# The modulation's products side by side in four column groups of TensorE, in float32

## The chip, the cores and the metric

The kernel runs on one core of one Trainium2 chip. The metric is the device time of one execution in microseconds (us), from the first to the last instruction and what lies around it. Engines are named as the profile names them: PE is TensorE's matmul, PEld its weight load, DVE is VectorE, ACT ScalarE, POOL GpSimd, SP the engine that issues the DMAs.

## The reference, cut to what matters

A network of two blocks runs over 256 rows of 1024 channels. The first block has two layers, a Hyena layer (gated long convolution by a Fourier transform) and an attention layer. Each layer is modulated by two conditioning vectors, one for the latent rows and one for the context rows:

```
sc_lat, sc_ctx = silu(c), silu(c_ctx)                     # 1024 numbers each
for i in range(2):
    sh, sc, gt       = split(sc_lat @ ada_w[i] + ada_b[i], 3)
    sh_c, sc_c, gt_c = split(sc_ctx @ ada_w[i] + ada_b[i], 3)
    h_lat = rms_norm(x_lat, g[i]) * (1 + sc) + sh         # the same for h_ctx with the _c parts
    x_lat = x_lat + gt * mixer(h_lat, ...)
```

`ada_w` is 2 x 1024 x 3072 in float32, 25 MB in all, so the modulation multiplies two rows by a large matrix. The second block (recurrences, window attention and a mixture of experts whose rows are gathered by index) takes the larger part of the time and isn't touched by the change.

## The kernel before, in words

The activations of the first block lie transposed in `hT`, eight chunks of 128 channels by 512 rows. Large products are made by three matmuls (`mm3`, lines 115 to 117) on operands that are split into a rounded part (`hi`, by ACT, line 77) and the rest (`lo`, by DVE or POOL, line 78), both read by TensorE in the type float32r. Each weight tile of 128 x 1024 (512 KB) comes by one DMA into a ring of four raw tiles `w` (`load`, line 93), and is split into a ring of three split tiles (`weights`).

The function `ada` makes the modulation of one layer in six column blocks `nb` of 512. A block takes four tiles of `ada_w` (`h` = 0 to 3), and each tile holds two chunks `c` of the 1024 input channels, so a block sums eight products in one PSUM bank. The stationary operand is the conditioning vectors' chunk, 128 x 2; the moving operand is the weight, 128 x 512. ACT copies the sum to `row`, TensorE turns it by four transposes, and DVE adds the bias into `mod0` (layer 0) or `mod1` (layer 1). `ada` gives control back after each tile, so that a caller can place one step of it between other work.

There are two ways through it:
- with `raws`: float32 matmuls straight from the raw tile, two columns (`cr`). Blocks 0 to 3 of layer 0 go this way ahead of the Hyena layer (raw tiles of their own, `aw`, 16 of them); so do blocks 3 to 5 of layer 1, at the end of the Hyena layer and behind it, out of the ring `w`.
- without: the weight is split as all others are, and the stationary operand `cs` has four columns (the two vectors' `hi` and `lo`). So a tile takes four float32r matmuls. Blocks 4 and 5 of layer 0 and blocks 0 to 2 of layer 1 go this way, one step (one tile) at a time between the products of the Hyena layer: the generator `aside`, 20 steps, called from `project(g + 1, (1,), ...)`.

Ahead of the Hyena layer `modulated` makes `hT` from `x`, `mod0` and the row norms, first for chunks 0 to 3 (it needs blocks 0 and 2), then for chunks 4 to 7 (blocks 1 and 3). Behind the Hyena layer the row norms of `x` are summed (`RmsRows.rows`), blocks 4 and 5 of layer 1 are finished, `modulated` makes `hT` for the attention layer, and its first products (keys and values, `at_kv`) follow.

The program isn't issued in the order in which it is written: the framework places instructions on each engine's queue by the order of the program as a priority and by a simulation of when each is ready. On the chip each queue then runs in that fixed order. All DMAs of weights are issued by SP, in order; one that has to wait for a free tile of a ring holds up those behind it.

Of the kernel before, what the change touches and what calls it, by code (L numbers as in the profile page):

```python
# [10 lines left out]
F32 = mybir.dt.float32  # L11
F32R = mybir.dt.float32r
# [3 lines left out]
AF = mybir.ActivationFunctionType  # L16
ALU = mybir.AluOpType
# [3 lines left out]
P = 128  # L21
D = 1024
NKD = D // P
# [125 lines left out]
def bc(ap, dim, n):  # L149

    v = ap.unsqueeze(dim)
    shape = list(v.shape)
    shape[dim] = n
    return v.broadcast_to(shape)
# [67 lines left out]
    nc.scalar.activation(out, x, AF.Sin)  # L222


def ada(k, io, l, cv, mod, nbs, rows, raws=None):

    nc = k.nc
    m = 2 if raws else 4
    for nb in nbs:
        ps = k.bank("A")
        for h in range(4):
            src = io["ada_w"][l, nb, h]
            w = (raws(src) if raws else k.weights(src, [2, 512]))
            for j in range(2):
                c = 2 * h + j
                if raws:  # L240
                    k.mm(ps[:2, :], cv[0][:, c, :], w[:, j * 512:(j + 1) * 512], c == 0, c == NKD - 1)
                else:
                    k.mm(ps[:4, :], cv[1][:, c, :], w.hi[:, j, :], c == 0, False)
                    k.mm(ps[:4, :], cv[1][:, c, :], w.lo[:, j, :], False, c == NKD - 1)
            if h < 3:
                yield
        row = rows([P, 512])[:m]
        nc.scalar.copy(row, ps[:m, :])
        pm = k.bank("B")
        for j in range(4):  # L250
            nc.tensor.transpose(pm[:, m * j:m * j + m], row[:, j * P:(j + 1) * P], k.ident[:m, :m])
        o = mod[:, 4 * nb:4 * nb + 4, :]
        pm = pm[:, :4 * m].rearrange("p (a b) -> p a b", b=m)
        nc.vector.tensor_tensor(o, pm[:, :, 0:2], bc(k.adab[:, l, 4 * nb:4 * nb + 4], 2, 2), ALU.add)
        if not raws:
            nc.vector.tensor_tensor(o, pm[:, :, 2:4], o, ALU.add)
        yield


# [1087 lines left out]
@with_exitstack  # L1347
def tile_model(ctx: ExitStack, tc: tile.TileContext, io, out):
    nc = tc.nc
    k = Kit(ctx, tc)  # L1350
    k.out = out
    k.ident = k.con.tile([P, P], F32, tag="ident", name="ident")
    make_identity(nc, k.ident)
    k.ones = k.con.tile([P, P], F32, tag="ones", name="ones")
    nc.vector.memset(k.ones, 1.0)
    k.half = k.con.tile([P, 1], F32, tag="half", name="half")
    nc.vector.memset(k.half, -0.5)
    banks = ExitStack()
    k.psum(banks, "1", {"A": 4, "B": 2, "C": 2})
    with ExitStack() as blk:  # L1360
        k.stage(blk, "1", 1024, 4, 3)
        b1 = blk.enter_context(tc.tile_pool(name="b1", bufs=1))
        x = b1.tile([P, NKD, 512], F32, tag="x", name="x")
        hT = k.new_split(b1, [P, NKD, 512], "hT1")
        cr = b1.tile([P, NKD, 2], F32, tag="cr", name="cr")
        nc.sync.dma_start(cr, io["cT"])
        cs = b1.tile([P, NKD, 4], F32R, tag="cs", name="cs")
        nc.scalar.activation(cr, cr, AF.Silu)
        nc.scalar.activation(cs[:, :, 0:2], cr, AF.Copy)
        nc.vector.tensor_tensor(cs[:, :, 2:4], cr, cs[:, :, 0:2].bitcast(F32), ALU.subtract)  # L1370
        mod0 = k.con.tile([P, 24, 2], F32, tag="mod0", name="mod0")
        mod1 = k.con.tile([P, 24, 2], F32, tag="mod1", name="mod1")
        ada_steps = lambda *a: ada(k, io, a[0], (cr, cs), *a[1:])

        def adas(*a):
            for _ in ada_steps(*a):
                pass

        with ExitStack() as c1:
            p1 = c1.enter_context(tc.tile_pool(name="hy", bufs=1))  # L1380
            hs = k.new_split(p1, [64, SEQ], "fhs")
            dft_f = k.new_split(p1, [P, 2, 2, 128], "dff")
            dft_i = k.new_split(p1, [P, 2, 2, P], "dfi")
            with ExitStack() as c2:
                fp = c2.enter_context(tc.tile_pool(name="filt", bufs=1))
                mlp = filter_mlp(k, fp, io, hs)
                rms = RmsRows(k, fp, 512)
                frow = lambda s: fp.tile(s, F32, tag="ada_row", name=k.uid("ada_row"))
                raws = lambda src: k.load(src, 1024, pool=fp)
                for i, _ in enumerate(ada_steps(0, mod0, (0, 2), frow, raws)):  # L1390
                    nc.sync.dma_start(x[:, i, :], io["xT"][:, i, :])
                    if i == 0:
                        k.adab = k.const(io["ada_b"], [P, 2, 24], "adab")
                        ng = k.const(io["norm_g"], [P, 2, NKD], "ng")
                    if i in (1, 3, 5):
                        next(mlp)
                    rms.add(x[:, i, :], fp.tile([P, 512], F32, tag="rms_q", name=k.uid("rms_q"), bufs=2))
                next(mlp, None)
                rb = rms.rows()
                adas(0, mod0, (1, 3), frow, raws)  # L1400
                modulated(k, fp, hT, x, mod0, ng[:, 0, :], rb, range(4))
                modulated(k, fp, hT, x, mod0, ng[:, 0, :], rb, range(4, 8))

            def load_dft():
                for d, n, w in ((dft_f, "dft_f", 512), (dft_i, "dft_i", 512)):
                    raw = k.raw.tile([P, 1024], F32, tag="w", name=k.uid("w"))[:, :w]
                    nc.sync.dma_start(raw, io[n])
                    k.split_into(d.view(lambda a: a.rearrange("p a b c -> p (a b c)")), raw)

            with ExitStack() as c2:  # L1410
                rms = RmsRows(k, p1, 512)

                hp = c2.enter_context(tc.tile_pool(name="hyg", bufs=1))
                hrow = lambda s: hp.tile(s, F32, tag="hcv", name=k.uid("ada_row"))

                def aside():
                    yield from ada_steps(0, mod0, range(4, 6), hrow)
                    yield from ada_steps(1, mod1, range(3), hrow)

                hyena(k, io, x, hT, hs, {}, dft_f, dft_i, mod0, hp, aside(), ada_steps(1, mod1, (3,), hrow, lambda src: k.load(src, 1024)), rms, load_dft)  # L1420
            with ExitStack() as c2:
                rp = c2.enter_context(tc.tile_pool(name="rm1", bufs=1))
                more = ada_steps(1, mod1, range(4, 6), lambda s: rp.tile(s, F32, tag="ada_row", name=k.uid("ada_row")), lambda src: k.load(src, 1024))
                for _ in range(3):
                    next(more)
                rb = rms.rows()
                for _ in more:
                    pass
                modulated(k, rp, hT, x, mod1, ng[:, 1, :], rb, range(NKD))
        with ExitStack() as c2:  # L1430
            at = c2.enter_context(tc.tile_pool(name="at", bufs=1))
            gqa(k, io, x, hT, mod1, at)
        k.iota = k.const(io["iota"], [P, P], "iota")
        k.tri = k.const(io["tri"], [P, P], "tri")
        k.msk = k.const(io["mask"], [P, 3, P], "msk")
        po = [k.bank("A") for _ in range(4)]
        for t in range(2):
            for dh in range(2):
                for j in range(4):
                    nc.tensor.transpose(po[2 * t + dh][:, j * P:(j + 1) * P], x[:, 4 * dh + j, t * P:(t + 1) * P], k.ident)  # L1440
    k.stage(ctx, "2", 1024, RAWS, 3)
    b2 = ctx.enter_context(tc.tile_pool(name="b2", bufs=1))
    h = [b2.tile([P, D], F32, tag=f"h{t}", name=f"h{t}") for t in range(2)]
    for t in range(2):
        for dh in range(2):
            nc.scalar.copy(h[t][:, dh * 512:(dh + 1) * 512], po[2 * t + dh])
    banks.close()
    k.psum(ctx, "2", {"G": 2, "M": 2, "C": 2, "D": 2})
    second = Second(k, io, b2, h)
    for t in range(2):  # L1450
        second.stats(t, 0, None)
        second.scaled(t)
    second.experts()
# [136 lines left out]
```

## Time and profile before

| what | value |
|---|---|
| runs before, median of 3 (lowest to highest) | 2750.16 us (2749.62 to 2754.34) |
| the profiled execution, its own time | 2752.02 us |
| its span, first to last instruction | 2750.3 us |
| PE busy over the span | 2364.6 us (86%) |
| DVE, ACT, POOL busy | 2075.2 (75%), 1294.2 (47%), 1055.5 us (38%) |
| mean granted TensorE clock | 0.958 |

The trace covers the whole span, 0 us being the first instruction. The stages that matter here: the prologue from 0 to about 44 us, the Hyena layer from there to about 610 us, the passage to the attention layer from 580 to 640 us. A busy share is a mean over a stage. The ends of matmuls are modelled, so that neighbours overlap in the records; the distance from start to start is what a matmul takes from TensorE.

### The profile page before, as it was taken

How to read it: one execution, taken by the hardware profiler on the slowest of the kernel's cores; microseconds unless marked ns; L12 is line 12 of the kernel's file. 1: busy time of each engine (PE TensorE's matmuls, PEld its weight loads, DVE VectorE, ACT ScalarE, POOL GpSimd, SP SyncE). 2: the span in 40 equal slices, each digit the busy share in tenths (PEclk: the TensorE clock that was granted, in tenths of full speed). 3: DMA queues.
4: the chain of work that ended last, by engine and by line, in shares of the span. 5: the costliest groups of instructions: out<-in, count | busy, mean ns of one | idle time of the engine just before them, and what ended most of it. 6: DMA issues, size and time to landing. Idle time of an engine off the chain costs nothing. (4 is left out here: it accounts for less than half of the span.)

```text
span 2750.3 us, 30013 instructions
## 1 busy us (share of the span) xinstructions
PE 2364.6 (86%) x8930; PEld 1463.6 (53%) x8930; DVE 2075.2 (75%) x4579; ACT 1294.2 (47%) x2960; POOL 1055.5 (38%) x844
## 2 busy tenths in 40 slices
PE   8999999999998786788978888987788998777776
PEld 4788888857888454445533344544344544322222
DVE  6788887766887876799758589867689966964444
ACT  4444444434554664467534366734366753322222
POOL 0322223221210443544445455544444454343332
PEclk9999999999999797899999999999999999899999
DMA  6333332224333554999899999999999999899997
GB/s 245 123 106 112 111 108 90 79 90 149 118 104 116 189 178 156 413 393 358 340 398 392 413 401 373 399 386 383 389 405 381 360 372 368 343 404 421 421 422 306
DMA packets 149162, 778.11 MB, mean 283 GB/s; under 512 B 18663, under 2 KB 19464, under 8 KB 83464
## 3 DMA queue, kind: packets, MB, share of 16 engines
q0 software_dynamic: 73728, 536.90, 48.2%
q1 hardware_dynamic: 75272, 239.29, 24.4%
q8 instruction: 72, 1.18, 0.2%
q14 instruction: 90, 0.74, 0.1%
HBM read 775.08 MB, written 1.05 MB: 282 GB/s over the span
## 5 line engine op out<-in xcount | busy, mean ns | idle before, releaser
L120 PE MATMUL psG<-uv,dg 128*128 128x512 f32 x2048 | 1009.5, 630 | 235.4 <-ACT dg L1281 235.0
L1267 DVE CUSTOM_DVE_ANT_0 uv<-uv,h 128x1024 f32<-128x1024 f32 x512 | 648.1, 1270 | 308.5 <-DMA uv<-in_peer_uv_dram,idx 303.9
L1258 POOL DMA_INDIRECT uv<-in_peer_uv_dram,idx x512 | 602.9, 1177 | 455.6 <-PE psG L120 266.9
L120 PEld LDWEIGHTS psG<-uv,dg 128*128 128x128 f32 x2048 | 387.9, 199 | 706.7 <-ACT dg L1281 349.8
L77 ACT ACTIVATE wh<-w 128x512 fp32r<-128x512 f32 (+3 forms) x644 | 454.0, 721 | 483.8 <-PE psA L116 178.7
L78 DVE TENSOR_TENSOR wl<-w,wh 128x512 fp32r<-128x512 f32 (+3 forms) x494 | 441.9, 909 | 126.5 <-ACT wh L77 123.3
L78 POOL TENSOR_TENSOR wl<-w,wh 128x512 fp32r<-128x512 f32 (+1 forms) x150 | 233.0, 1554 | 541.5 <-issue 362.9
L1271 ACT ACTIVATE cf<-act 128x2 f32<-128x2 f32 x256 | 51.7, 202 | 545.2 <-DVE act L1267 544.6
L117 PE MATMUL psA<-hT1h,wl 128*128 128x512 f32 (+1 forms) x640 | 235.7, 369 | 2.4 <-DVE wl L78 2.4
L115 PE MATMUL psA<-hT1h,wh 128*128 128x512 f32 (+1 forms) x640 | 236.9, 371 | 0.0
L116 PE MATMUL psA<-hT1l,wh 128*128 128x512 f32 (+1 forms) x640 | 235.6, 368 | 0.0
L116 PE MATMUL psM<-wl,hTh 128*128 128x512 f32 (+1 forms) x352 | 180.5, 513 | 42.2 <-DVE wl L78 37.0
L115 PE MATMUL psM<-wh,hTh 128*128 128x512 f32 (+1 forms) x352 | 169.6, 484 | 22.9 <-DVE idx L689 12.8
L1281 ACT ACTIVATE dg<-ident,cf 128x128 f32<-128x128 f32 x512 | 174.9, 386 | 1.0 <-PE psG L120 1.0
L117 PE MATMUL psM<-wh,hTl 128*128 128x512 f32 (+1 forms) x352 | 142.6, 405 | 0.0
L115 PEld LDWEIGHTS psA<-hT1h,wh 128*128 128x128 f32 x640 | 120.6, 188 | 23.4 <-issue 0.9
L117 PEld LDWEIGHTS psA<-hT1h,wl 128*128 128x128 f32 x640 | 120.5, 188 | 23.1 <-DVE wl L78 2.8
L116 PEld LDWEIGHTS psA<-hT1l,wh 128*128 128x128 f32 x640 | 120.6, 188 | 19.9
L116 PEld LDWEIGHTS psM<-wl,hTh 128*128 128x128 f32 x352 | 71.3, 203 | 106.7 <-DVE wl L78 60.1
L1278 ACT ACTIVATE cf<-cf,gate 128x1 f32<-128x1 f32 x512 | 122.3, 286 | 6.6
L369 POOL TENSOR_TENSOR hm<-hx,hx 128x512 f32<-128x512 f32 x16 | 30.5, 1905 | 187.5 <-ACT hx L359 187.5
L115 PEld LDWEIGHTS psM<-wh,hTh 128*128 128x128 f32 x352 | 70.8, 202 | 57.1 <-issue 23.3
(417 smaller groups left out, 3813.9 us busy)
## 6 DMA issues: line engine op xcount, KB each, us to landing
w<-in_w_in_r_dram SPq DMA_DIRECT2D x128, 512.0 KB, 7.9
w<-in_hy_w_in_dram SPq DMA_DIRECT2D x64, 512.0 KB, 3.5
w<-in_w_out_dram SPq DMA_DIRECT2D x64, 512.0 KB, 6.0
w<-in_ada_w_dram SPq DMA_DIRECT2D x32, 512.0 KB, 3.5
w<-in_peer_wq_dram SPq DMA_DIRECT2D x32, 512.0 KB, 7.8
lng<-in_ln_gb_dram SPq DMA_DIRECT2D x40, 256.0 KB, 5.6
aw<-in_ada_w_dram SPq DMA_DIRECT2D x16, 512.0 KB, 8.6
w<-in_hy_w_out_dram SPq DMA_DIRECT2D x16, 512.0 KB, 3.5
```

The source lines that it names most:

```text
L77: nc.scalar.activation(dst.hi, src, AF.Copy)
L78: (eng or nc.vector).tensor_tensor(dst.lo, src, dst.hi.bitcast(F32), ALU.subtract)
L115: mm(out, a.hi, b.hi, start=start, stop=False)
L116: mm(out, a.hi, b.lo, start=False, stop=False)
L117: mm(out, a.lo, b.hi, start=False, stop=stop)
L120: self.nc.tensor.matmul(out, a, b, start=start, stop=stop)
L369: nc.gpsimd.tensor_tensor(m[:, ci, :], got[0], got[3], ALU.mult)
L1258: nc.gpsimd.indirect_dma_start(out=uv.rearrange("p a b -> p (a b)"), out_offset=None, in_=self.io[f"peer_uv{n // 2}"], in_offset=bass.Indi ...
L1267: nc.vector.tensor_tensor_reduce(u, u, self.h[i // P % 2], 1.0, 0.0, ALU.mult, ALU.add, acts[i // 2][:, i % 2:i % 2 + 1])
L1271: nc.scalar.activation(cfs[b], acts.pop(b), AF.Gelu)
L1278: nc.scalar.activation(cf[:, j:j + 1], cf[:, j:j + 1], AF.Copy, scale=gate[:, c:c + 1])
L1281: nc.scalar.activation(dg, k.ident, AF.Copy, scale=cf[:, j:j + 1])
```

## The change

Every block now goes by the raw tile, in float32. The stationary operand `cr` is widened to 32 columns, of which 30 are zeros. Chunk `c` writes to the 32 partitions from `c % 4 * 32` of the PSUM bank, that is to one of four column groups of TensorE, and each group sums two chunks (`c` and `c + 4`). So the bank holds four partial sums, of which two rows each are used. The row copy takes all 128 partitions. In place of the transposes there are four float32 matmuls with the copied rows as stationary operand (128 x 128) and `four` (128 x 2) as moving operand: it holds ones at rows 0, 32, 64 and 96 for the first vector, and one row further for the second, so that the product adds up the four partial sums and turns them at once.

```
-    m = 2 if raws else 4
...
-            w = (raws(src) if raws else k.weights(src, [2, 512]))
+            w = raws(io["ada_w"][l, nb, h])
             for j in range(2):
                 c = 2 * h + j
-                if raws:
-                    k.mm(ps[:2, :], cv[0][:, c, :], w[:, j * 512:(j + 1) * 512], c == 0, c == NKD - 1)
-                else:
-                    k.mm(ps[:4, :], cv[1][:, c, :], w.hi[:, j, :], c == 0, False)
-                    k.mm(ps[:4, :], cv[1][:, c, :], w.lo[:, j, :], False, c == NKD - 1)
+                q = c % 4 * 32
+                k.mm(ps[q:q + 32, :], cr[:, c, :], w[:, j * 512:(j + 1) * 512], c < 4, c >= 4)
...
-        row = rows([P, 512])[:m]
-        nc.scalar.copy(row, ps[:m, :])
+        row = rows([P, 512])
+        nc.scalar.copy(row, ps)
         pm = k.bank("B")
         for j in range(4):
-            nc.tensor.transpose(pm[:, m * j:m * j + m], row[:, j * P:(j + 1) * P], k.ident[:m, :m])
+            k.mm(pm[:, 2 * j:2 * j + 2], row[:, j * P:(j + 1) * P], k.four)
...
-        if not raws:
-            nc.vector.tensor_tensor(o, pm[:, :, 2:4], o, ALU.add)
...
+        c2s = b1.tile([P, NKD, 2], F32, tag="c2s", name="c2s")
+        nc.sync.dma_start(c2s, io["cT"])
+        cr = b1.tile([P, NKD, 32], F32, tag="cr", name="cr")
+        nc.vector.memset(cr, 0.0)
+        nc.scalar.activation(cr[:, :, 0:2], c2s, AF.Silu)
+        k.four = b1.tile([P, 2], F32, tag="four", name="four")
+        nc.vector.tensor_tensor(k.four, k.ident[:, 0:2], k.ident[:, 32:34], ALU.add)
+        for q in (64, 96):
+            nc.vector.tensor_tensor(k.four, k.four, k.ident[:, q:q + 2], ALU.add)
...
-                    yield from ada_steps(0, mod0, range(4, 6), hrow)
-                    yield from ada_steps(1, mod1, range(3), hrow)
+                    yield from ada_steps(0, mod0, range(4, 6), hrow, lambda src: k.load(src, 1024))
+                    yield from ada_steps(1, mod1, range(3), hrow, lambda src: k.load(src, 1024))
```

The operand `cs` and its split go. The steps, their order in the program and the DMAs stay as they were.

## Rows read from the trace of the kernel before

**Rows 1.** Busy time by stage: engines' busy us (instructions), granted clock, DMA share, GB/s.
```profile
75.00:110.00 35.00, 35.00 (x167) 28.02 (x166) 25.80 (x35) 14.92 (x20) 8.99 (x6) 1.00 0.32 109
...
285.00:320.00 35.00, 35.00 (x165) 28.29 (x164) 29.37 (x46) 13.12 (x18) 12.31 (x8) 1.00 0.28 95
...
580.00:620.00 40.00, 33.70 (x122) 16.01 (x122) 25.44 (x52) 12.38 (x21) 6.10 (x5) 1.00 0.31 105
```

**Rows 2.** By operand: the matmuls that read `cs`, then those that read `cr` from `w`.
```profile
L120 PE MATMUL psA<-wh,cs x40: 387/397/478, 72.9 to 364.4; 128*4 128x512 f32 x40
...
L120 PE MATMUL psA<-w,cr x48: 589/592/592, 582.0 to 626.9; 128*2 128x512 f32 x48
```

**Rows 3.** Order of time on PE in the Hyena layer (start, us, instructions), one step of `aside`.
```profile
72.89 0.40 PE L120 MATMUL psA<-wh,cs 128*4 128x512 f32 x1
...
73.58 0.40 PE L120 MATMUL psA<-wl,cs 128*4 128x512 f32 x1
73.82 0.39 PE L115 MATMUL psA<-hT1h,wh 128*128 128x512 f32 x1
```

**Rows 4.** Order of time on PE at the Hyena layer's end: one float32 matmul of two columns.
```profile
588.12 0.40 PE L117 MATMUL psC<-hsph,dfil 128*128 128x512 f32 x1
588.45 1.02 PE L120 MATMUL psA<-w,cr 128*2 128x512 f32 x2
589.40 0.72 PE L115 MATMUL psC<-hsph,dfih 128*128 128x512 f32 x2
589.96 0.40 PE L116 MATMUL psC<-hspl,dfih 128*128 128x512 f32 x1
```

**Rows 5.** Order of time on PE, second block: float32 matmuls of 128 and of 64 columns.
```profile
1263.25 1.16 PE L120 MATMUL psC<-tri,da 128*128 128x128 f32 x8
...
1294.22 0.66 PE L120 MATMUL psD<-la,avv 128*64 128x128 f32 x8
```

**Rows 6.** Order of time on PE, passage to the attention layer.
```profile
610.39 5.31 PE L120 MATMUL psA<-w,cr 128*2 128x512 f32 x12
615.63 1.05 PE L120 MATMUL psB<-ones,rms_a 128*128 128x1 f32 x8
616.61 1.02 PE L120 MATMUL psA<-w,cr 128*2 128x512 f32 x2
...
620.94 0.41 PE L251 MATMUL psB<-ident,ada_row 2*128 2x2 f32 x4
621.27 6.17 PE L120 MATMUL psA<-w,cr 128*2 128x512 f32 x14
627.38 0.98 PE L115 MATMUL psA<-wh,hT1h 128*128 128x512 f32 x3
```

**Rows 7.** Groups by line and shape, 0 to 330 us: the split's second half on DVE.
```profile
L78 DVE TENSOR_TENSOR wl<-w,wh 128x1024 fp32r<-128x1024 f32 x59 | 82.1, 1393 | 26.3 <-ACT wh L77 25.0 <-PE psA L120 1.4
```

**Rows 8.** Order of time in the prologue: PE, then DVE.
```profile
42.62 0.50 PE L115 MATMUL psA<-hT1h,wh 128*128 128x512 f32 x1
...
30.20 1.26 DVE L201 SCALAR_TENSOR_TENSOR mod_t<-x,modA,psB 128x256 f32<-128x256 f32 x3 [1.51 <-PE psB L120]
...
37.80 2.36 DVE L78 TENSOR_TENSOR wl<-w,wh 128x1024 fp32r<-128x1024 f32 x2 [0.21 <-ACT wh L77]
44.20 0.17 DVE L254 TENSOR_TENSOR mod<-psB,adab 128x8 f32<-128x8 f32 x1 [4.04 <-PE psB L251]
```

**Rows 9.** Order of time in the passage: DVE, ACT, SP's issues.
```profile
613.19 0.69 DVE L171 TENSOR_TENSOR rms_a<-rms_a,ht 128x512 f32<-128x512 f32 x1 [0.76 <-ACT ht L170]
...
626.19 1.06 ACT L77 ACTIVATE wh<-w 128x1024 fp32r<-128x1024 f32 x1 [1.73 <-DMA w<-in_at_kv_dram]
...
622.33 14.09 SPq L93 DMA_DIRECT2D w<-in_at_kv_dram  x6
```

**Rows 10.** Busy time by stage around the passage to the second block, columns as in rows 1.
```profile
885.00:895.00 10.00, 2.40 (x21) 2.00 (x19) 7.51 (x19) 3.32 (x9) 2.57 (x3) 0.87 0.50 171
...
905.00:910.00 5.00, 4.31 (x13) 2.98 (x12) 4.81 (x27) 2.56 (x7) 1.94 (x2) 0.55 0.81 277
```

More of the change, by code (lines that the diff above doesn't have):

```diff
@@ L222, in sine, with ada @@
     nc.scalar.activation(out, x, AF.Sin)
-def ada(k, io, l, cv, mod, nbs, rows, raws=None):
+def ada(k, io, l, cr, mod, nbs, rows, raws):
     nc = k.nc
-    m = 2 if raws else 4
     for nb in nbs:
@@ L235, in ada @@
         for h in range(4):
-            src = io["ada_w"][l, nb, h]
-            w = (raws(src) if raws else k.weights(src, [2, 512]))
+            w = raws(io["ada_w"][l, nb, h])
             for j in range(2):
                 c = 2 * h + j
-                if raws:
-                    k.mm(ps[:2, :], cv[0][:, c, :], w[:, j * 512:(j + 1) * 512], c == 0, c == NKD - 1)
-                else:
-                    k.mm(ps[:4, :], cv[1][:, c, :], w.hi[:, j, :], c == 0, False)
-                    k.mm(ps[:4, :], cv[1][:, c, :], w.lo[:, j, :], False, c == NKD - 1)
+                q = c % 4 * 32
+                k.mm(ps[q:q + 32, :], cr[:, c, :], w[:, j * 512:(j + 1) * 512], c < 4, c >= 4)
             if h < 3:
                 yield
-        row = rows([P, 512])[:m]
-        nc.scalar.copy(row, ps[:m, :])
+        row = rows([P, 512])
+        nc.scalar.copy(row, ps)
         pm = k.bank("B")
         for j in range(4):
-            nc.tensor.transpose(pm[:, m * j:m * j + m], row[:, j * P:(j + 1) * P], k.ident[:m, :m])
+            k.mm(pm[:, 2 * j:2 * j + 2], row[:, j * P:(j + 1) * P], k.four)
         o = mod[:, 4 * nb:4 * nb + 4, :]
-        pm = pm[:, :4 * m].rearrange("p (a b) -> p a b", b=m)
-        nc.vector.tensor_tensor(o, pm[:, :, 0:2], bc(k.adab[:, l, 4 * nb:4 * nb + 4], 2, 2), ALU.add)
-        if not raws:
-            nc.vector.tensor_tensor(o, pm[:, :, 2:4], o, ALU.add)
+        nc.vector.tensor_tensor(o, pm[:, :8].rearrange("p (a b) -> p a b", b=2), bc(k.adab[:, l, 4 * nb:4 * nb + 4], 2, 2), ALU.add)
         yield
@@ L1364, in tile_model @@
         hT = k.new_split(b1, [P, NKD, 512], "hT1")
[L1365 to L1370, printed above, removed]
+        c2s = b1.tile([P, NKD, 2], F32, tag="c2s", name="c2s")
[7 more added lines that the diff above has]
+            nc.vector.tensor_tensor(k.four, k.four, k.ident[:, q:q + 2], ALU.add)
         mod0 = k.con.tile([P, 24, 2], F32, tag="mod0", name="mod0")
         mod1 = k.con.tile([P, 24, 2], F32, tag="mod1", name="mod1")
-        ada_steps = lambda *a: ada(k, io, a[0], (cr, cs), *a[1:])
+        ada_steps = lambda *a: ada(k, io, a[0], cr, *a[1:])
         def adas(*a):
```

## The prediction

> **What bounds the kernel now.** I read the busy time by stage first, then the order of time on PE in each stage that the change touches, then DVE's, ACT's and SP's around the places where PE stands still. In the Hyena layer PE is busy 35.00 of 35 us in stage after stage while DVE has 25.8 to 29.4 us and ACT 13 to 15 [rows 1]. Start to start, the matmuls there lie 0.23 us apart without a hole [rows 3]. So from about 44 to 580 us each 0.1 us that PE gets more or less to do is 0.1 us of the end, and work taken from ACT and DVE is worth nothing. In the passage to the attention layer PE isn't full (33.70 of 40 us, [rows 1]): there a chain decides. In the prologue PE reaches the first product of the Hyena layer at 42.62 us, and DVE has just stood idle for 4.04 us until the turned modulation came [rows 8]. The change touches all three places. What comes behind 640 us is shifted and not changed.
>
> **The unit.** Float32r matmuls have one record: 40 for 20 steps of two `hi` products. Float32 ones have two: 48 for three blocks of eight products [rows 2]. A two-column float32 matmul of 512 runs 588.45 to 589.40, 0.95 us for two records; the full-width record before it takes 0.33 us from start to start instead of 0.23, and the two full-width records behind it 0.56 instead of 0.46 [rows 4]. In a run of them a record takes (615.63 - 610.39) / 12 = 0.43 us [rows 6]. So a visit of TensorE to the narrow float32 shape costs about 0.30 us (0.10 on the way in, 0.95 - 0.86 = 0.09 on the way out, 0.10 for the first weights behind it) beside 0.43 us a record.
>
> **Do the column groups run side by side?** No row shows four groups of 32, but two of 64 are there: eight records of 64 columns take 0.66 us, eight of 128 columns at the same 128 moving columns take 1.16 us [rows 5]. In the source the 64-column products stand as four records of one half and then four of the other. A quarter of the 0.43 us record is 0.107 us for 128 columns; one after another, eight would need seven starts of 0.107 and a tail of about 0.27 us, 1.02 us. In 0.66 us there is room for half of the starts. So both halves ran together, although one stands behind the other in the queue. I take the same for two groups of 32: the two products of one tile cost the time of one. The other end is no overlap, four records of 0.43 us.
>
> The Trainium skill (TensorE: Matmul & The Clock Gate, Part 3, "Measured speedup vs the span model") says that matmuls start and end strictly in program order. By that rule the second product's first record could not start ahead of the first product's second one, and a pair would take three records. The 0.66 us above doesn't agree with it: in that order the last of eight would start six records in, and 0.91 us be needed. By the rule the Hyena term below would be 20 x (3 x 0.43 + 0.30 - 0.93) = +13.2 us instead of +4.6, and the forecast some 9 us higher.
>
> **Hyena layer, 20 steps.** A step now takes 72.89 to 73.82, 0.93 us for four records, with no loss on either side [rows 3]. After: two records' time and one visit, 0.86 + 0.30 = 1.16 us. That is +0.23 us, 20 times: +4.6 us. With no overlap: 1.72 + 0.30 - 0.93 = 1.09, +21.8 us. Where a step comes to lie beside another float32 product of narrow shape the visit is shared: the low end is +2.
>
> **The turn, 12 blocks.** Four transposes take 620.94 to 621.27, 0.33 us [rows 6]. The new matmuls load 128 columns of float32 and move two; the nearest row is the norm's sum (128 columns, one moving): eight records in 615.63 to 616.61, 0.98 us. So +0.65 us a block. For the five blocks inside the Hyena layer PE pays it: +3.3 us. In the prologue and the passage PE has holes; there I count nothing, at most 2 us.
>
> **What is removed.** Twenty splits, on DVE 1.39 us each (28 us, [rows 7]) and on ACT as many instructions. PE doesn't wait for either in that layer, so nothing. Should PE find itself waiting, this would be the gain. The raw tile of a step is now held until PE has read it instead of until it is split; the next load into that tile of the ring then starts when PE goes on to the next weight, 24 matmuls of 0.23 us = 5.5 us of work, with one more split weight behind it. I take no stall. The row copy, the smaller bias add and the few instructions that make `four` and `cr` lie off the path: nothing.
>
> **Prologue.** The 28 records of blocks 1 and 3 that run just ahead of 42.62 (14 for each, 0.43 us a record) shrink to a quarter or half and end with the loads, before the norms are ready at 30.20. DVE's 4.04 us of idle time ahead of 44.20 then goes [rows 8]. What PE waits for next is the first weight split, 37.80 + 1.2 = 39.0 us; its `hi` part comes a little earlier. I take a start at 38.5 instead of 42.62: -4.1 us. But PE then stands still from about 31 to 38 us. Where it had little to do, 2.40 us of 10, the granted clock fell to its lower level, 1.2 of 2.4 GHz, and it stood at a mean of 0.55 still in the stage from 905 to 910 [rows 10]. At the lower level a record takes twice as long; three to seven us of it cost 1.5 to 3.5 us. I take 2. Sum: -2, between -7 (PE starts as soon as a few chunks and weights are there, clock kept) and +4 (the first rival).
>
> **Passage.** The norm's sums start at 615.63 though DVE had their input at 613.88 (613.19 + 0.69): PE was in 12 records of block 4 [rows 6, 9]. These become three pairs, 2.6 us, done at 613.0. So the sums and all that hangs on them move by 1.7 us. The first key product, at 627.38, hangs on another chain: its load is issued at 622.33, once the ring's tile is free of block 5's first products, and 5.05 us later, over landing and split (626.19 + 1.06), PE begins [rows 6, 9]. Block 5's first tile then is read some 3.8 us earlier (block 4 shorter, norms earlier): issue at 618.5, start at 623.5. I take -4 us, between -1 (turn and visits eat it, or the clock falls here too) and -7 (the tile is read ahead of the norms).
>
> **Sum.** -2 + 4.6 + 3.3 - 4 = +1.9 us on the profiled execution's 2752.02 us (span 2750.3), which lies 1.9 us over the runs' median; so 2752 for the median. A change under 0.2%, 5.5 us, is about what a measurement of this kernel can't tell from none.
>
> **Rivals.**
> - *The splits fall behind.* With blocks 1 and 3 early, the second half of `modulated` is ready when the first ends, and has priority over the first weights' splits. DVE's first half took 30.20 to about 37.6; two halves end at 45.0, a split at 46.2, and PE starts 3.6 us later than before instead of 4.1 earlier. For it: DVE had room for the splits only because it waited [rows 8]. Against: a gap of DVE suffices to let one in. It decides once PE's start passes 42.6 us. Sum 3.6 + 7.9 - 4 = +7.5 us: 2758, slower. Chance 0.20.
> - *The pair is slower than one.* No overlap for 32 columns gives 21.8 + 3.3 and nothing in the other two places: +25, 2775; chance 0.07. Order kept strictly, as in the page's rule, 13.2 + 3.3 - 2 - 3 = +11.5: 2762; chance 0.06. Against both: [rows 5].
> - *The visits are cheaper than they look.* Two steps of `aside` come to lie next to each other, since they need no split any more; then four groups share 0.86 us and one visit: 10 x (1.16 - 1.86) = -7 instead of +4.6, and the sum is -9.7: 2740.5, faster. For it: the framework reorders. Against: each step stands behind a product of its own in the program. With the prologue at -7 and the passage at -7 the sum is -6.1 even without it. Both together 0.20.
> - The forecast itself, within 5.5 us: 0.47.
>
> The range: 2743 takes in most of the faster case, 2763 the first rival and the strict order. Faster 0.20, within 0.2% 0.47, slower 0.33.
>
> **What would show it.** In the Hyena layer, `cr` records of 32 columns in twos with starts a few ns apart, a step of 1.16 us from first start to the next full-width product, less one visit's entry; turns of about 1 us. In the prologue, the first full-width product at 38 to 39 us and a clock below 1.00 there; above 42.6 the first rival holds. In the passage, the norm's sums at 613.9 and the first key product near 623.5. I am wrong if the pair's four records follow each other by 0.43 us, if PE shows holes in the Hyena layer, or if the order of DVE's work in the prologue turns.

## The result: slower by 0.9%, and where the time went

The changed kernel takes 2772.97 us in the median of 6 runs (2766.94 to 2780.11), the kernel before, run beside it, 2748.66. The ratio is 1.0091, 95% interval 1.0069 to 1.0112: 24 to 25 us slower, where +2 us were forecast. Its profiled execution has a span of 2771.9 us and a mean granted clock of 0.947.

To place the 21.6 us between the spans I take starts of the same product in both traces:

| stretch, from one start to the next | before | after | difference |
|---|---|---|---|
| 0 to the 33rd `psA<-hT1h,wh` (prologue and the first products) | 67.3 | 77.2 | +9.9 |
| to the 501st (the Hyena layer) | 488.2 | 495.9 | +7.7 |
| to the 513th, the first behind the keys and values (passage) | 130.7 | 140.7 | +10.1 |
| to the last product of the second block (`psG<-uv,dg`) | 2052.0 | 2046.0 | -6.0 |

The last line isn't the change's. The second block is the same in all runs below, and from execution to execution its stretch differs from the one in the table's first column by -14.7 to +6.8 us; in e7, which reaches the 513th product within 1.1 us of before, by -9.1. So the profiled execution of before was rather long there, and the first three lines tell what the change did.

**The Hyena layer is what the sum said.** Order of time on PE around one step of `aside` and one turn in the changed kernel, then the group by operand, to lay beside [rows 2, 3]:
```profile
82.51 0.39 PE L117 MATMUL psA<-hT1h,wl 128*128 128x512 f32 x1
82.83 1.05 PE L120 MATMUL psA<-w,cr 128*32 128x512 f32 x4
83.81 0.50 PE L115 MATMUL psA<-hT1h,wh 128*128 128x512 f32 x1
...
106.14 1.03 PE L120 MATMUL psB<-four,ada_row 128*128 128x2 f32 x8
...
L120 PE MATMUL psA<-w,cr x128: 589/593/1063, 82.8 to 642.6; 128*32 128x512 f32 x128
```
Four float32 records of a step lie between 82.83 and 83.81: 0.98 us, where four one after another would need 1.72. With 0.32 instead of 0.23 us ahead of them and 0.10 more behind, a step costs 1.17 us. A turn takes 0.89 us (106.14 to the next start, 107.03).

**The prologue lost its order.** PE first, then DVE, to lay beside [rows 8]:
```profile
26.86 1.87 PE L120 MATMUL psB<-four,ada_row 128*128 128x2 f32 x8 [0.70 <-ACT ada_row L243]
29.99 1.87 PE L120 MATMUL psB<-ones,rms_a 128*128 128x1 f32 x8 [1.27 <-DVE rms_a L171]
31.79 1.91 PE L120 MATMUL psA<-aw,cr 128*32 128x512 f32 x2
33.63 2.08 PE L120 MATMUL psB<-ident,rms_r 128*128 128x128 f32 x8
35.63 2.18 PE L120 MATMUL psA<-aw,cr 128*32 128x512 f32 x14
...
40.24 1.92 PE L120 MATMUL psA<-aw,cr 128*32 128x512 f32 x16
...
44.11 0.50 PE L115 MATMUL psA<-hT1h,wh 128*128 128x512 f32 x1
...
48.08 0.79 PE L115 MATMUL psA<-hT1h,wh 128*128 128x512 f32 x1 [3.24 <-ACT wh L77]
...
52.44 0.80 PE L117 MATMUL psA<-hT1h,wl 128*128 128x512 f32 x1 [2.19 <-DVE wl L78]
53.03 0.63 PE L115 MATMUL psA<-hT1h,wh 128*128 128x512 f32 x1
53.46 0.63 PE L116 MATMUL psA<-hT1l,wh 128*128 128x512 f32 x1
```
```profile
28.76 0.17 DVE L248 TENSOR_TENSOR mod<-psB,adab 128x8 f32<-128x8 f32 x1 [0.78 <-PE psB L120]
...
29.25 0.69 DVE L171 TENSOR_TENSOR rms_a<-rms_a,rms_q 128x512 f32<-128x512 f32 x1
...
35.74 1.26 DVE L201 SCALAR_TENSOR_TENSOR mod_t<-x,modA,psB 128x256 f32<-128x256 f32 x3 [3.69 <-PE psB L120]
...
44.24 0.17 DVE L248 TENSOR_TENSOR mod<-psB,adab 128x8 f32<-128x8 f32 x1 [1.10 <-PE psB L120]
...
44.85 1.66 DVE L201 SCALAR_TENSOR_TENSOR mod_t<-x,modA,psB 128x256 f32<-128x256 f32 x4
...
51.16 3.49 DVE L78 TENSOR_TENSOR wl<-w,wh 128x1024 fp32r<-128x1024 f32 x3
```
Three things are to be seen.

- The order on DVE. The idle gap ahead of the second half of `modulated` has shrunk from 4.04 us to 1.10, and the half goes through in one piece. The first weights' splits, which stood in that gap at 37.80, now stand behind the half, at 51.16.
- Which side the gap closed from. What the second half waits for isn't early: the bias add of block 3 comes at 44.24, where it came at 44.20 before. PE makes the products of blocks 1 and 3 between 31.79 and 42.16, around and behind the norm's spread. The first half of `modulated` is late: it begins at 35.74 instead of 30.20 and ends at 43.1 instead of 37.6. The sum of the last chunk's squares stands behind the turn's bias add on DVE, and turn, sums and spread take 1.87, 1.87 and 2.08 us; the sums' eight records took 0.98 in [rows 6].
- What PE pays. It makes its first product at 44.11, 1.5 us later than before, and then waits 3.24 us for a `hi` part and 2.19 for a `lo` part. Its records of this time stand about 0.43 us apart (53.03 to 53.46) instead of 0.23, until 56.4. That is about 3 us more, the rest of the +9.9.

**The passage did the same.** PE, DVE and SP, to lay beside [rows 6, 9]:
```profile
632.23 1.02 PE L120 MATMUL psA<-w,cr 128*32 128x512 f32 x2 [2.84 <-DMA w<-in_ada_w_dram]
633.18 1.56 PE L120 MATMUL psB<-ones,rms_a 128*128 128x1 f32 x8
...
646.13 1.20 PE L115 MATMUL psA<-wh,hT1h 128*128 128x512 f32 x4 [0.70 <-ACT wh L77]
655.94 0.79 PE L116 MATMUL psA<-wl,hT1h 128*128 128x512 f32 x1 [8.61 <-DVE wl L78]
...
653.88 0.47 DVE L201 SCALAR_TENSOR_TENSOR mod_t<-x,modA,psB 128x256 f32<-128x256 f32 x1
654.67 1.22 DVE L78 TENSOR_TENSOR wl<-w,wh 128x1024 fp32r<-128x1024 f32 x1
...
636.61 19.66 SPq L93 DMA_DIRECT2D w<-in_at_kv_dram  x5
```
The first key weight's `hi` part is there and four products start at 646.13; the fifth needs the `lo` part, which DVE makes at 654.67, behind all eight chunks of `modulated`: PE waits 8.61 us. The stages show the price in both places (busy time by stage; columns as in [rows 1]):
```profile
30.00:38.00 8.00, 7.82 (x32) 4.17 (x32) 2.68 (x8) 1.31 (x3) 1.04 (x1) 0.61 1.03 406
44.00:54.00 10.00, 4.57 (x12) 2.68 (x13) 9.65 (x22) 5.25 (x11) 0.00 (x0) 0.62 0.11 24
...
640.00:660.00 20.00, 9.96 (x35) 5.41 (x36) 15.99 (x36) 10.19 (x19) 0.00 (x0) 0.59 0.35 129
```
Before, PE was busy 10.00 of 10 and 20.00 of 20 us in the last two, at a granted clock of 1.00; here it has 4.57 and 9.96 us, at 0.62 and 0.59.

### The profile page after: what moved, and what is told of

Same layout as the page of the kernel before. It is cut to its first block, busy times and chain, and to the rows that moved or that the text cites. A ratio compares the mean times of both kernels' runs of the same rounds, so it can differ in the third digit from the quotient of the medians.

```text
span 2771.9 us, 30036 instructions
## 1 busy us (share of the span) xinstructions
PE 2371.2 (86%) x8978; PEld 1471.8 (53%) x8978; DVE 2040.4 (74%) x4557; ACT 1276.2 (46%) x2939; POOL 1044.1 (38%) x844
## 3 DMA queue, kind: packets, MB, share of 16 engines
HBM read 775.08 MB, written 1.05 MB: 280 GB/s over the span
## 5 line engine op out<-in xcount | busy, mean ns | idle before, releaser
L77 ACT ACTIVATE wh<-w 128x512 fp32r<-128x512 f32 (+2 forms) x624 | 433.3, 710 | 494.7 <-PE psA L116 183.4
L78 DVE TENSOR_TENSOR wl<-w,wh 128x512 fp32r<-128x512 f32 (+3 forms) x474 | 413.7, 888 | 132.6 <-ACT wh L77 130.8
L116 PE MATMUL psM<-wl,hTh 128*128 128x512 f32 (+1 forms) x352 | 181.1, 514 | 41.0 <-DVE wl L78 35.5
```

The costliest lines, as they stand in the source:

```text
L77: nc.scalar.activation(dst.hi, src, AF.Copy)
L78: (eng or nc.vector).tensor_tensor(dst.lo, src, dst.hi.bitcast(F32), ALU.subtract)
L116: mm(out, a.hi, b.lo, start=False, stop=False)
```

## The experiments

All numbers of stretches are against the kernel before, in us, from the profiled execution, cut as in the table above; the ratio is that of the timed runs with its 95% interval.

| run | prologue | layer | passage | ratio |
|---|---|---|---|---|
| the change | +9.9 | +7.7 | +10.1 | 1.0091 [1.0069, 1.0112] |
| e1 groups in the layer alone | +1.1 | +7.8 | -0.3 | 1.0029 [1.0012, 1.0046] |
| e2 groups at the ends alone | +12.3 | +0.3 | +11.9 | 1.0079 [1.0052, 1.0106] |
| e3 splits first | +8.1 | +7.7 | +2.9 | 1.0057 [1.0030, 1.0083] |
| e4 two tiles a visit | +11.3 | +8.8 | +8.4 | 1.0098 [1.0061, 1.0136] |
| e5 two filling products a tile | +21.3 | +7.7 | +11.4 | 1.0143 [1.0119, 1.0167] |
| e6 e3 and the norm's sum first | +6.8 | +7.7 | +1.1 | 1.0060 [1.0038, 1.0082] |
| e7 before, splits first | -0.2 | 0.0 | -0.9 | 0.9994 [0.9980, 1.0008] |
| e8 ends alone, mended as e6 | +6.3 | +0.3 | +2.7 | 1.0023 [1.0005, 1.0041] |
| e9 e8 and one filling product | +15.6 | +0.3 | +2.7 | 1.0034 [1.0017, 1.0050] |
| e10 layer alone, every second visit | -0.6 | -4.5 | +0.2 | 0.9964 [0.9948, 0.9981] |
| e11 e9 and e10 together | +12.0 | -4.0 | -0.2 | 1.0020 [1.0004, 1.0035] |
| e12 e8, products repeated | +5.1 | +0.3 | +2.8 | 1.0010 [0.9997, 1.0024] |
| e13 e12, PE's waits filled | +4.2 | +0.3 | +3.2 | 0.9994 [0.9976, 1.0011] |
| e14 e13 and e10 together | +2.7 | -4.3 | -0.1 | 0.9988 [0.9971, 1.0004] |

The theory after the comparison: DVE's order at both ends costs most (the first rival, at two places), the late norm chain the rest of the prologue, and the layer costs 7.7, where 7.9 were forecast. Its rival: the column groups cost it themselves, by visits, turns and clock.

**e1 and e2, one part alone.** `ada` of before is kept as `ada_old` and called at the ends (e1) or in `aside` (e2).
```
e1: -  ... ada_steps(0, mod0, (0, 2), frow, raws)      + ... old_steps(0, mod0, (0, 2), frow, raws)   (and blocks 1, 3; 3 to 5)
e2: -  yield from ada_steps(1, mod1, range(3), ...)    + yield from old_steps(1, mod1, range(3), hrow)  (and blocks 4, 5)
```


> Column groups only in the 20 steps inside the Hyena layer (and the new turn of their five blocks); prologue and passage go the way of before. Both theories of the two ends (order of DVE's splits; lower clock) expect nothing there: the first full-width product at 42.6 us and the 160th at the same place as before, the Hyena layer longer by 20 x 0.23 + 5 x 0.65 = 7.9 us (7.5 measured in the changed kernel), the key products 7 to 8 us later than before. Total about +7.5 us on before, ratio 1.0027. A third theory, that the whole change disturbs a ring or a queue beyond its place, expects more than +12.

> Column groups only in the prologue (blocks 0 to 3 of layer 0) and in the passage (blocks 3 to 5 of layer 1); the 20 steps in the Hyena layer by split weights as before. If the changed kernel's three losses add up: +10 us by the time the layer's second stretch begins (77 instead of 67 us), none inside the layer, +10 in the passage, total about +17 to +20 us, ratio 1.006 to 1.007. If the loss at the ends came from the steps (their raw tiles held longer), it would be gone: ratio 1.000.


The parts hardly touch each other: the layer has its +7.8 without the ends, and the ends cost +12.3 and +11.9 without the layer.

**e3, the order on DVE.** The first three weights of the Hyena layer and of the keys are loaded and split ahead of `modulated` in the program.
```
+                early = {p: k.weights(io["hy_w_in"][0, p], [NKD, P]) for p in (1, 2, 0)}
                 modulated(k, fp, hT, x, mod0, ng[:, 0, :], rb, range(4))
...
+                early_kv = [k.weights(io["at_kv"][0, h], [2, 512]) for h in range(3)]
                 modulated(k, rp, hT, x, mod1, ng[:, 1, :], rb, range(NKD))
```


> The changed kernel, but the first three weights of the Hyena layer and of the keys are split ahead of the modulation in the program, so that DVE's queue has them earlier. Order theory: the loss in the passage goes from +10 to about +1 (first split of a key weight some 10 us earlier than 654.67), the one in the prologue from +10 to about +5 (what is left is the norm chain's 5.5 us of delay): 14 us less than the changed kernel, ratio to before about 1.004. Clock theory (TensorE at its lower level is what makes both ends late, and the splits only fill the time): at most 2 us less than the changed kernel, ratio 1.008 or more.


The first key split on DVE, and the PE product that waits for it:
```profile
645.38 1.22 DVE L78 TENSOR_TENSOR wl<-w,wh 128x1024 fp32r<-128x1024 f32 x1
...
646.66 0.80 PE L116 MATMUL psA<-wl,hT1h 128*128 128x512 f32 x1 [1.08 <-DVE wl L78]
```
PE's wait is 1.08 us instead of 8.61, and the passage costs 2.9 instead of 10.1: there, the order was the cause. In the prologue only 1.8 us come back. There the norm chain was later still in e3: its turn came at 28.54 instead of 26.86, the turn ahead of that had already run at half rate (1.87 us at 17.27), and the first scaled chunk came at 37.4.

**e7, the same order in the kernel before.**
```
 the two additions of e3, on the kernel before
```


> The kernel before, with nothing changed but the order: the first three projection weights and the first three key weights stand ahead of the scaling. Before, two of the first splits already lie between the two halves of the scaling, so the first stretch should move by 0 to -2 us; in the passage the first key product waits for the first key-weight split at the same 0.1 us, so 0 to -3 us: 0.998 to 1.000. The rival: the splits take VectorE's time from the scaling, and the first products come 2 to 4 us later: 1.001 to 1.003.


There is nothing to be measured, and none of the three stretches moves by 1 us. So the early splits are worth something only to the changed kernel: they give back what it lost.

**e4 and e10, four groups at a time.** In e4 a step of `aside` loads and multiplies two tiles, at ten places instead of twenty. In e10 (on e1) each step loads one tile, and every second step multiplies two.
```
e4:  -            if h < 3:          +            if h in stops:        # (1,) in the Hyena layer
e10: +            ws.append((h, raws(io["ada_w"][l, nb, h])))
     +            for h2, w, j in [(*hw, j) for hw in ws for j in range(2)] if len(ws) == per else ():   # per = 2
```


> The changed kernel, but a step in the Hyena layer takes two weight tiles, so that four groups run in one visit, 10 visits instead of 20. If four groups of 32 columns overlap as two do and a visit costs 0.30 us whatever is in it: 0.86 + 0.30 = 1.16 us for two tiles, 11.6 us less in the layer than the changed kernel's 23.2 us, which makes the layer some 4 us shorter than before; total some 11 us under the changed kernel, ratio to before about 1.005. If only two groups run at a time: 1.72 + 0.30 = 2.02 us for two tiles, 3 us less. If the cost isn't the visit: no change, 1.009.

> Column groups in the Hyena layer alone (e1), with a tile loaded at every visit, as there, but multiplied at every second visit, two tiles together in four groups: 10 visits of 1.00 us instead of 20 of 0.98, and no visit that asks for two tiles. If the run with two tiles at a visit (e4) gave its 9.7 us back because two tiles at once stood ahead of the projection's weights in the ring of raw tiles, the gain stays here: the Hyena layer takes 486 us from the 33rd to the 501st of its first products, against 496.0 in e1, 495.9 in the changed kernel and 488.2 before, and the time is 0.999 to 1.000. If it was the missing fill of TensorE's waits by the other ten visits, the layer stays at 493 or above, and the time at 1.002 or more.


Four groups do run together. Eight records in e4 and the next start, then PE and ACT half a layer block on:
```profile
84.31 1.07 PE L120 MATMUL psA<-w,cr 128*32 128x512 f32 x8
85.31 0.50 PE L115 MATMUL psA<-hT1h,wh 128*128 128x512 f32 x1
...
139.89 0.79 PE L115 MATMUL psC<-hsph,dfih 128*128 128x512 f32 x1 [1.99 <-ACT hs L403]
...
137.33 1.06 ACT L77 ACTIVATE wh<-w 128x1024 fp32r<-128x1024 f32 x1 [3.46 <-DMA w<-in_hy_w_in_dram]
...
139.25 0.59 ACT L403 COPY hs<-psC 128x512 f32<-128x512 f32 x1
```
1.00 us for eight records, and so all visits together 9.96 us instead of 19.65; yet e4's layer isn't shorter. The weight tile of the projection landed late, ACT waited 3.46 us for it to split it, the copy of a PSUM bank stood behind that split on ACT, and PE waited for the copy. The two tiles of a step stand ahead of that weight in the ring of four. Waits of this kind come to 6.1 us of PE in the layer (the largest 3.4). The visits save 9.7 us, and the layer is 1.1 us longer than the change's, so some 10.8 us are lost; the other 4.7 go with a lower granted clock behind the waits (0.89 from 215 to 250 us, where the change has 1.00), which no run takes apart from them. In e10, with one load a step, PE has no such wait in the whole layer:
```profile
77.78 1.07 PE L120 MATMUL psA<-w,cr 128*32 128x512 f32 x8
78.78 0.50 PE L115 MATMUL psA<-hT1h,wh 128*128 128x512 f32 x1
```
The layer takes 483.7 us (486 were expected), 4.5 less than before and 12.2 less than in the change. The rival, that ten places were left without their fill, falls, since e10 leaves them empty too. e10 is faster than both kernels, by 0.36% against before: 10 us, in an interval of 5 to 14. Its stretches up to the 513th product show 5.0 of them, the layer 4.5; where the other 5 come from, if they aren't chance, no stretch tells.

**e6 and e8, the norm's sum first.** e6 is e3 with the eighth chunk of `x` loaded, squared and summed one step earlier, ahead of the second block's turn. e8 is the same with `aside` as before.
```
-                    nc.sync.dma_start(x[:, i, :], io["xT"][:, i, :])
+                    for c in ((i,), (6, 7), ())[max(i - 5, 0)]:
+                        nc.sync.dma_start(x[:, c, :], io["xT"][:, c, :])
```


> The kernel with the splits first (e3), and the eighth chunk's square and sum put ahead of the second block's turn in the program. If the norm chain is late because that sum stands behind the turn on ScalarE and VectorE, the norm sums start at 28.5 us or before instead of 30.0 to 31.8, the first scaled chunk comes at 35 or before instead of 37.4, and the first stretch (to the 33rd of the first products) ends at 73 instead of 75.4: 1.005. If the clock alone makes it late, nothing moves by over 1 us, and it stays at 1.0057.

> The column groups in the first stretch and the passage only, steps by split weights, splits first, and the eighth chunk's sum ahead of the turn. If what the ends cost was the order on VectorE and ScalarE, the first stretch goes from +12.3 us to +6 and the passage from +11 to +2: 1.002 to 1.003, and below e2's 1.0079 in any case. If the ends cost it by the column groups themselves (their drain, their turns, the clock), it stays within 3 us of e2: 1.007.


The sum no longer stands behind the turn. Against e3, where the turn comes as late (28.54), the sums start 1.6 us earlier (30.11 instead of 31.67) and the first chunk 2.0 (35.44 instead of 37.43). Against the change they start no earlier (30.1 and 30.2 to 29.99), since the turn comes later there. e6's ratio can't be told from e3's; its prologue gains 1.3 us. e8 came out as expected for an order that was mended, +6.3 and +2.7.

**e5, e9, e12, e13, what PE's half rate costs.** Products that nobody reads are added in the prologue. e5 (on the change) and e9 (on e8): two and one full-width product of each tile. e12 (on e8): every product of blocks 0 and 2 made twice in its own 32 columns. e13 (on e12): full-width products in three of PE's waits.
```
e5:  +            for j in range(2 if busy else 0):                   # e9: range(1 ...
     +                k.mm(k.bank("C"), k.ident, w[:, j * 512:(j + 1) * 512], True, True)
e12: +                k.mm(dump[q:q + 32, :], cr[:, c, :], w[:, j * 512:(j + 1) * 512], True, True)
e13: +                    if i == 5:
     +                        for _ in range(4):
     +                            k.mm(k.bank("C"), k.ident, x[:, 0, :], True, True)   # and one behind each row copy, two behind the sums
```


> The changed kernel, with two full-width float32 products of each raw tile against the identity added in the first stretch, into a bank that nobody reads: TensorE does about as much there as before the change. If the late norm chain is the clock's doing, the granted clock of 20 to 38 us goes from 0.5 to 0.6 back above 0.9, the norm sums take 1.05 us instead of 1.87 and the rows' spread 1.16 instead of 2.08, the first scaled chunk comes at 33.5 us or before instead of 35.7, and the first stretch gives back 2 to 3 us; the order on VectorE is not touched, so the first weight splits still stand behind both halves, and the whole is at 1.008. If the chain is late by the order of the work alone, the clock rises and the first scaled chunk stays at 35.7 or later, and the time stays at 1.009 or above.

> The kernel with the ends mended (e8), with one full-width float32 product of each raw tile against the identity in the first stretch, into a bank that nobody reads. In e8 the turn, the norm sums and the rows' spread took 1.87, 1.85 and 2.08 us where they take 1.05, 1.05 and 1.05 in the run with two such products. If TensorE's half rate is what is left of the late chain, these go to 1.05 each, the first scaled chunk comes at 32 to 33 us instead of 35.5, the first stretch ends at 71 instead of 73.6 and the time is 1.0010 to 1.0015. If the half rate costs nothing that is waited for, or the one product fills what it gives back, it stays at 1.002 or above.

> The kernel with the ends mended (e8), where each product of the first two blocks is made twice, the second time in the same 32 columns and into a bank that nobody reads: TensorE has more to do while the norm chain is made, and nothing full-width stands between the groups. If TensorE's half rate holds the chain up, the turn, the norm sums and the rows' spread take 1.05, 1.05 and 1.16 us instead of 1.87, 1.85 and 2.08, the first scaled chunk comes at 31 to 33.5 us instead of 35.5, the first stretch ends at 70 to 72 instead of 73.6, and the time is 1.0005 to 1.0015. If the repeats themselves hold the chain up (they stand ahead of it in TensorE's order), or the rate stays halved, the first scaled chunk comes at 35.5 or later and the time is 1.0023 or above.

> The run with the first two blocks' products made twice (e12), with full-width float32 products that nobody reads put into TensorE's three waits there: four ahead of the last product of the filter's small network (a wait of 2.34 us), one behind each of the first two blocks while their rows are copied (0.66), two behind the norm sums (1.37). If TensorE's half rate is what is left, the turn, the sums and the spread take 1.05, 1.05 and 1.16 us instead of 1.87, 1.85 and 2.08, the first scaled chunk comes at 31 to 32 us instead of 34.1, the first stretch ends at 69 to 70 instead of 72.4 and the time is 1.000 against 1.0010. If the chain is late by its order, the three get short and the chunk stays at 33.5 or later.


e5 keeps the granted clock at 1.00 from 14 to 56 us and the sums and the spread at 1.05 us, but its products hold up what they were to help: first chunk at 41.9. Both theories missed its price, and e9's, for one reason. PE in e9:
```profile
27.05 1.05 PE L120 MATMUL psA<-aw,cr 128*32 128x512 f32 x4
28.04 1.12 PE L120 MATMUL psC<-aw,ident 128*128 128x512 f32 x2
29.09 1.05 PE L120 MATMUL psA<-aw,cr 128*32 128x512 f32 x4
```
A tile and its filling product take 2.04 us: 0.98 up to the filling product, and 1.05 for it. Sixteen records of column groups in a row, four tiles, take 1.92 in the changed kernel's 40.24 to 42.16, 0.48 a tile, and a filling product among its like takes 0.91 (eight records in 3.63 us, 23.07 to 26.70 in e13). So a full-width product between the tiles costs mainly because each pair then runs alone and takes as long as four groups together (0.98 against 1.00 us), and for some 0.14 us through the visit. e12, which parts nothing, costs nothing and brings the chunk from 35.5 to 34.1, but the rate still falls (0.50 from 30 to 38 us). In e13 it doesn't, there. The chain in e8, then in e13 with its stretches:
```profile
28.48 1.87 PE L120 MATMUL psB<-four,ada_row 128*128 128x2 f32 x8 [0.70 <-ACT ada_row L243]
30.21 1.85 PE L120 MATMUL psB<-ones,rms_a 128*128 128x1 f32 x8
33.42 2.08 PE L120 MATMUL psB<-ident,rms_r 128*128 128x128 f32 x8 [1.37 <-POOL rms_r L124]
...
35.54 1.26 DVE L201 SCALAR_TENSOR_TENSOR mod_t<-x,modA,psB 128x256 f32<-128x256 f32 x3 [2.66 <-PE psB L120]
```
```profile
30.22 0.95 PE L120 MATMUL psB<-four,ada_row 128*128 128x2 f32 x8
31.03 1.03 PE L120 MATMUL psB<-ones,rms_a 128*128 128x1 f32 x8
...
33.72 1.05 PE L120 MATMUL psB<-ident,rms_r 128*128 128x128 f32 x8
...
34.81 1.26 DVE L203 SCALAR_TENSOR_TENSOR mod_t<-x,modA,psB 128x256 f32<-128x256 f32 x3 [1.02 <-PE psB L120]
...
46.25 0.80 PE L117 MATMUL psA<-hT1h,wl 128*128 128x512 f32 x1 [2.04 <-DVE wl L78]
...
30.00:38.00 8.00, 7.29 (x51) 4.60 (x51) 4.99 (x16) 3.23 (x7) 1.04 (x1) 1.00 1.00 396
...
44.00:54.00 10.00, 7.96 (x28) 6.31 (x28) 10.00 (x20) 6.79 (x12) 0.00 (x0) 0.72 0.33 98
```
From the turn to the first chunk it is 4.6 us (30.22 to 34.81) instead of 7.1 (28.48 to 35.54): so the half rate costs this chain 2.5 us. The chunk itself comes 0.7 us before e8's and 0.7 after e12's, since the four products ahead of the small network take 3.70 us where PE had waited 2.34: the expected 31 to 32 was missed for that. What is left of the prologue is +4.2: the start (43.01 instead of 42.62) 0.4, a wait of 2.04 us for DVE's `lo` part at 46.25 (DVE is busy 10.00 of 10 us from 44 to 54), and records that stand 0.43 us apart until 49.77, the rest of about 1.8 (granted clock 0.72 in that stage). The profiled execution of e13 is the longest of its 12 runs, as is e9's, so the ratios say more than their stretches.

**e11 and e14, everything together.** e11 is the change with the mends of e6, one filling product and the visits of e10; e14 has the fillings of e13 instead.
```
+                    yield from ada_steps(1, mod1, range(3), hrow, lambda src: k.load(src, 1024), False, 2)
```


> The changed kernel with all mends: splits first, the eighth chunk's sum ahead of the turn, one filling product a tile in the first stretch, and two tiles' products at every second visit in the Hyena layer. If the costs add up as in the single runs: the ends as in the run with one filling product, the layer as in the run with every second visit, so 1.000 to 1.002, against 1.0091 for the change as made. If the mends get in each other's way, it stays above 1.004.

> Column groups at all places, with every mend that helped: splits first, the eighth chunk's sum ahead of the turn, the waits of the first stretch filled, two tiles' products at every second visit in the Hyena layer. If the parts add up: the first stretch +2 to +5 us and the passage +3 as with the filled waits, the layer -4.5 as in e10, so 0.999 to 1.001. The rival, that they get in each other's way as in e11: 1.002 or above.


The layer's gain is in both (-4.0, -4.3) and stands beside what the ends cost: e11 has e9's dear prologue, e14 lies 0.0002 below what was expected and can't be told from the kernel before. Their passages, -0.2 and -0.1, beat e13's +3.2 in the same order. The traces show PE at another rate there: in e13 a turn at 631.87 takes 1.87 us and a block's last twelve records 3.63, at a granted clock of 0.50, in e14 1.05 and 1.91 at 0.66 to 0.83. Why it is granted more in e14 no run shows, and e14's profiled execution is the shortest of 12. Groups at the ends bring nothing that shows, even mended; in the layer alone, with two tiles a visit, the kernel gains 0.36%, of which the stretches show half.

## Why the prediction was wrong

**Right: the side-by-side run, the unit and the layer.** Two groups of 32 ran together in 0.98 us, a step cost 1.17 (1.16 said), the layer +7.7 (7.9 said, 4.6 + 3.3): the turns 2.8 of it (4.47 us for 40 records instead of 1.68 for 20), the visits the rest. Nor was the raw tile's longer hold a stall.

The Trainium skill (TensorE: Matmul & The Clock Gate, Part 3, "The mechanism") has matmuls start and end strictly in program order. What the prediction worked out from it, 13.2 + 3.3 us for the layer, didn't come: it measured 7.7. The rule itself isn't refuted by that. A pair's four records start at 82.825, 82.832, 83.279 and 83.285, so the two products take turns; whether the queue already holds them so, or TensorE lets them pass, the trace doesn't show. That one product stands whole behind the other in the queue was taken from the source.

**Wrong: the prologue's term, -2, measured +9.9.** The first step that failed is that the records of blocks 1 and 3 "shrink to a quarter or half and end with the loads, before the norms are ready at 30.20". They shrank, but PE made them from 31.79 to 42.16, behind the sums and around the spread, and DVE's gap closed because the first half of `modulated` came 5.5 us late, not because its second half came early. The second is "What PE waits for next is the first weight split, 37.80 + 1.2 = 39.0 us": that place was taken over from the trace of before, and the split now stands at 51.16. The first rival had this order, and it decided, as said, past 42.6 (44.11). That it came true is in part luck, for its reason, blocks 1 and 3 early, didn't hold; what the framework's simulation expected when it placed the splits, no run shows. Its price was too low as well (3.6), for it let `modulated` begin at 30.20.

The 5.5 us of the first chunk can be divided, from single executions. Before, the chain began here:
```profile
26.24 0.41 PE L251 MATMUL psB<-ident,ada_row 2*128 2x2 f32 x4
```
From the turn's start to the first chunk it took 3.96 us before, 8.88 in the change, 7.06 in e8 and e12, where the last chunk's sum is out of the turn's way and the rate is still half, and 4.59 in e13, where the rate is full. From e3 to e6, the other pair of runs that differ in that order, it falls as much (8.89 to 7.05). So the order was worth 1.8 us, the half rate 2.5, the longer turn and what else there is 0.6; the turn itself began 0.6 later. The prediction had counted 2 us for the rate, but in PE's own records; those came as well (about 3 us, up to 56.4), and the chain on top.

The Trainium skill (TensorE: Matmul & The Clock Gate, Part 1, "HAM oscillation — how this bites in real kernels") says that gaps in TensorE's work set its clock back to the lower level. The traces agree in direction. Before, PE was busy 9.16 of the 10 us from 20 to 30, at a granted clock of 1.00; in the changed kernel 5.95, with waits of up to 2.08 us, and the granted clock was 0.50, its lower level (1.2 of 2.4 GHz), with 0.61 from 30 to 38. With the waits filled (e13) turn, sums and spread took 0.95, 1.03 and 1.05 us.

**Wrong: the passage's term, -4, measured +10.1.** Of its steps the load came 2.8 us earlier than the layer's end did (636.61, 14.3 later than before, against 17.1 by the first product of block 4, 627.47 instead of 610.39), where 3.8 was said. The sums didn't come 1.7 earlier but 0.5 later, behind a pair whose tile PE waited 2.84 us for. But the step that failed is "5.05 us later, over landing and split, PE begins": it gave the split no queue. From the load's issue (636.61) to the first key product (646.13) it took 9.5 us, since ACT made the `hi` part at 645.04, behind a row copy and a part of `hT`, and then PE waited 8.61 us more for the `lo` part, behind eight chunks on DVE. The same order that the first rival put a price on in the prologue wasn't asked for here, and e3 shows it to be 7.2 of the 10.1.

**The rival on the cheaper visits.** Two steps never came together by themselves. Made to share a visit, without crowding the ring, they give 12.2 us (e10), about the -11.6 that the rival had worked out (from +4.6 to -7).

## What to carry to other kernels

When a change makes one engine's work on a chain shorter, ask for each operation that stood in the other engines' gaps where it goes when the gap closes. It can close from either end, because the work behind it comes early or, as here, because the work ahead of it comes late; in both cases the queue's fixed order may put the operation behind both. Ask it at every place with that pattern, not only at the first. Small matmuls in column groups are paid by the visit and not by the matmul: gather as many groups as there are before going there, but spread their loads. And an engine that gets less to do may do the little that is left on the critical chain at half its rate.

## What the runs showed of the hardware that was not expected

- Four column groups cost what two do: eight float32 records of 512 in 1.00 us (e4, 84.31 to 85.31), four in 0.98 (82.83 to 83.81 in the change); sixteen in a row 1.92, by the modelled end of the last.
- A full-width product between column groups costs more than its own records: 2.04 us for a tile with one (e9), of which 0.98 are the pair that now runs alone and 0.91 the product, where a tile among its like takes 0.48. The Trainium skill (TensorEngine Tiling (Array Packing), "Key Properties") says that a change of tiling mode drains the engine. The trace agrees as far as it goes: around a pair in the changed kernel it shows 0.32 instead of 0.23 us ahead and 0.10 more behind.
- The granted clock in the records isn't always the whole story: in e6 it reads 1.00 from 30 to 38 us, while the norm sums took 1.84 us at 30.11 and the spread 2.08, twice what they take in e13 (e8 the same, 1.85 and 2.08). Durations of known operations were the surer sign.
